# The first projections of a two-layer backbone on one Trainium2 core, with TensorE's order in that stage written out by hand

## The chip, the cores and the metric

The kernel runs on one core of one Trainium2 chip. A core has five engines that work side by side, each through a queue of its own: TensorE (PE, matrix products), VectorE (DVE), ScalarE (ACT), GpSimd (POOL) and SyncE (SP), which in this kernel issues every transfer between memory and the core. An instruction starts when the one ahead of it on its engine has gone and when what it reads and the buffer it writes are free. What counts is the time of one execution on the chip in microseconds (us).

## What is computed

Two layers work on 512 latent and 256 context tokens of 2048 features. Each begins with a normalisation whose scale and shift come from a product of a conditioning vector with a large matrix (the modulation), and then one wide input projection:

```python
for l in range(DEPTH):
    mod = silu_c @ w_mod[l] + b_mod[l]
    shift, scale, gate = jnp.split(mod[:, None, :], 3, axis=-1)
    cmod = silu_cc @ w_mod[l] + b_mod[l]
    cshift, cscale, cgate = jnp.split(cmod, 3)
    h = rmsnorm(x, norm_g[l]) * (1.0 + scale) + shift
    hc = rmsnorm(cx, norm_g[l]) * (1.0 + cscale) + cshift
    if l % 2 == 0:
        u = h @ e_w_in[i]
        uc = hc @ e_w_in[i]
        ...
        y1, yc1 = mixer_a(ua, uca, cs64, lam, lam_init, a_sub_g[i], with_ctx)
        y2, yc2 = mixer_b(ub, ucb, cs128, b_sink[i], with_ctx)
    ...
    y = jnp.concatenate([y1, y2], axis=-1) * jax.nn.silu(ug)
    x = x + gate * (y @ w_o[l])
```

The change lies in the first layer, between the loading of `x` and the first attention head of `mixer_a`: there shift and scale of all 2048 features are needed before `h` is, and four columns of the projection are computed while `h` comes into being. `w_mod[0]` alone is 50 MB.

## The kernel before

The token matrix is held with the features on the 128 partitions: 16 chunks of 128 features, each 128 x 768 (512 latent tokens, then 256 context tokens). All products are float32 worth of precision made of three passes: an operand is split into a rounded part h and a rest l, and `mm_step` (L272) forms h·wh, l·wh and h·wl for the latent columns (512 wide) and the context columns (256 wide), six matmuls in all.

**The first stage** works in eight groups g, each of two chunks, 2g and 2g+1.

- *Modulation of a group*, `mod_first(g)` (L134): shift and scale of 256 features for both conditioning vectors. Its 4.2 MB of weights come in eleven pieces of 384 KB (the last of 256 KB), each loaded on SP's queue (L140) into a buffer called `mraw0`. From each, TensorE makes three narrow matmuls (L144, 32 x 256; 64 rows of the trace to a group) into one accumulator bank T. After the last, ScalarE copies T to an SBUF tile e (L149), four short pairs of matmuls with the constant `sel` pick and add up the result (L151; "the selection", eight rows of the trace), and VectorE adds the bias and forms the scale (`mod_finish`, L125 and L129).
- *h of a chunk*, `make_h` (L342): xn = x times the norm's factor (L348; on VectorE for every third chunk, else on GpSimd), h on ScalarE (L353), then on VectorE the unrounded value (L356) and the rest l (`sub`, L218). It needs the group's shift and scale.
- *Four projected columns* at once (`A_K0`, `A_Q0`, `A_V0`, `E_G0`): four steps of `mm_step` to a chunk, into banks J, J, J, O for the latent tokens and halves of S for the context. Their sums stay open over all 16 chunks. Weights come for four chunks at a time in four pieces of 256 KB (`wraw`, L268; three buffers, and the tile `macc` for the fourth), are rounded by ScalarE (`wh`, L259) and their rest made by VectorE (`wl`, L218), four buffers each.

The pieces `mraw0` live in buffers of two pools: `hslot`, where the h and l of all chunks will be (32 tiles, free until a chunk needs them), for groups 0 to 4, and `slot` (11 tiles), where x lies until its chunk has been normalised, for groups 5 to 7.

**Background work.** The rest of `w_mod` (gates of the first layer, everything of the second) is computed by `mod_later` (L154): 512 KB pieces `mraw` (two buffers of the pool `wp`), multiplied and added up by VectorE (L173) or by ScalarE and GpSimd (L170, L171) in one accumulator `macc`. The generator `later` is advanced by calls of `tick` at many places of the program.

**What sets the order.** The program text is only the dependence order: a scheduler with a timing model places each engine's instructions when the kernel is built, and each engine then runs its list strictly in that order. SP's list holds the transfers, so one whose buffer isn't free yet holds up all behind it. `tc.issue_after(x)` lets the scheduler place an instruction only once x has been placed; `tc.manual_schedule(engines=...)` keeps the named engines' instructions in the order in which the text writes them, within its block. The kernel before has no such block.

## Time and profile before

| | |
|---|---|
| three executions | 2575.84, 2571.32, 2575.29 us; median 2575.29 |
| the profiled execution | 2573.45 us, its span 2571.7 us |
| busy share of the span | TensorE 94%, VectorE 63%, ScalarE 44%, GpSimd 20% |
| moved from and to memory | 297.5 MB, 116 GB/s on average; 326 and 251 GB/s in the first two fortieths of the span |

The page of the profile gives the busy time of each engine over the span, the span in 40 slices of 64 us, and groups of instructions by line. A row of the trace in order of time reads: start, length, engine, line, operation, output<-inputs, tile sizes, how many instructions the row holds, and in brackets how long the engine had been idle before and which instruction ended that. "SPq" rows are transfers that SP issues; a row of waits (engine's queue, line, releaser: total, count, longest) says for what the queue stood still. A row of windows gives, for a stretch of time, each engine's busy time, the clock granted to TensorE (1.00 is full), the share of time that the DMA engines were busy, and GB/s.

### The profile page before, as it was taken

How to read it: one execution, taken by the hardware profiler on the slowest of the kernel's cores; microseconds unless marked ns; L12 is line 12 of the kernel's file. 1: busy time of each engine (PE TensorE's matmuls, PEld its weight loads, DVE VectorE, ACT ScalarE, POOL GpSimd, SP SyncE). 2: the span in 40 equal slices, each digit the busy share in tenths (PEclk: the TensorE clock that was granted, in tenths of full speed). 3: DMA queues.
4: the chain of work that ended last, by engine and by line, in shares of the span. 5: the costliest groups of instructions: out<-in, count | busy, mean ns of one | idle time of the engine just before them, and what ended most of it. 6: DMA issues, size and time to landing. Idle time of an engine off the chain costs nothing.

```text
span 2571.7 us, 36748 instructions
## 1 busy us (share of the span) xinstructions
PE 2427.3 (94%) x14214; PEld 2088.3 (81%) x14214; DVE 1608.2 (63%) x2720; ACT 1128.6 (44%) x2143; POOL 517.6 (20%) x340
## 2 busy tenths in 40 slices
PE   4889999999999999999999999899999999999998
PEld 2667888988788888878878888688888888887787
DVE  4367666656865787877666554857735325776534
ACT  3244444544554554544343332444434334554434
POOL 1132001101400354353303442310010001000010
PEclk9899999999999999999999999899999999999999
DMA  9762111111312233342334554535522222222234
GB/s 326 251 216 74 48 50 56 56 55 57 105 53 69 90 133 124 107 145 97 118 127 153 183 182 138 205 106 170 178 70 79 78 83 70 62 87 70 92 117 148
DMA packets 99087, 297.51 MB, mean 116 GB/s; under 512 B 11616, under 2 KB 12640, under 8 KB 98912
## 3 DMA queue, kind: packets, MB, share of 16 engines
q1 hardware_dynamic: 98912, 295.16, 34.5%
q8 instruction: 112, 1.84, 0.3%
q14 instruction: 63, 0.52, 0.1%
HBM read 269.16 MB, written 25.95 MB: 115 GB/s over the span
## 4 chain that ended last, share of the span: by engine, by line
PE 51%; DVE 7%; issue 2%; ACT 2%; DMA 2%; POOL 1%; ACTq 0%; SPq 0%; DVEq 0%; POOLq 0%
PE J L278 13%; PE J L279 13%; PE J L281 13%; PE O L533 4%; PE S L477 2%; DVE macc L173 2%; PE T L518 2%; DMA mraw<-in_wm_dram 2%; PE S L473 2%; DVE wl L218 1%; POOL macc L171 1%; DVE l L359 1%; DVE mc L489 1%; PE J L181 1%; PE T L243 0%
## 5 line engine op out<-in xcount | busy, mean ns | idle before, releaser
L278 PE MATMUL J<-h,wh 128*128 128x512 f32 (+1 forms) x2224 | 791.3, 359 | 23.8 <-ACT h L353 13.4
L279 PE MATMUL J<-l,wh 128*128 128x512 f32 (+1 forms) x2224 | 769.0, 356 | 4.7 <-DVE l L359 2.7
L281 PE MATMUL J<-h,wl 128*128 128x512 f32 (+1 forms) x2224 | 709.1, 356 | 2.8 <-DVE wl L218 2.8
L218 DVE TENSOR_TENSOR wl<-wraw,wh 128x512 fp32r<-128x512 f32 x500 | 402.2, 809 | 348.2 <-ACT wh L259 326.6
L259 ACT CAST wh<-wraw 128x512 fp32r<-128x512 f32 x492 | 302.4, 618 | 545.2 <-PE J L279 472.1
L278 PEld LDWEIGHTS J<-h,wh 128*128 128x128 f32 x2224 | 424.7, 192 | 104.7 <-ACT h L353 14.5
L279 PEld LDWEIGHTS J<-l,wh 128*128 128x128 f32 x2224 | 426.1, 192 | 62.6 <-DVE l L218 3.9
L281 PEld LDWEIGHTS J<-h,wl 128*128 128x128 f32 x2224 | 390.6, 192 | 38.8 <-DVE wl L218 5.1
L171 POOL TENSOR_TENSOR macc<-macc,mraw 128x512 f32<-128x512 f32 x180 | 267.9, 1489 | 254.1 <-ACT mraw L170 226.6
L278 PE MATMUL J<-yh,wh 128*128 128x512 f32 (+1 forms) x800 | 276.6, 352 | 5.1 <-ACT yh L441 5.1
L279 PE MATMUL J<-yl,wh 128*128 128x512 f32 (+1 forms) x800 | 272.8, 351 | 1.0 <-DVE yl L218 0.9
L173 DVE SCALAR_TENSOR_TENSOR macc<-mraw,silc,macc 128x512 f32<-128x512 f32 x240 | 241.7, 1007 | 42.3 <-DMA mraw<-in_wm_dram 38.6
L281 PE MATMUL J<-yh,wl 128*128 128x512 f32 (+1 forms) x800 | 253.2, 350 | 0.0
L489 DVE TENSOR_REDUCE mc<-S 128x1 f32<-128x768 f32 (+3 forms) x208 | 166.1, 799 | 137.9 <-PE S L477 88.1
L170 ACT ACTIVATE mraw<-mraw,silc 128x512 f32<-128x512 f32 x180 | 129.4, 723 | 192.4 <-DVE macc L173 171.6
L522 ACT CAST pth<-T 128x256 fp32r<-128x256 f32 (+2 forms) x288 | 124.9, 450 | 160.6 <-PE T L518 157.3
L278 PEld LDWEIGHTS J<-yh,wh 128*128 128x128 f32 x800 | 150.9, 190 | 32.8 <-ACT yh L441 5.9
L279 PEld LDWEIGHTS J<-yl,wh 128*128 128x128 f32 x800 | 151.1, 189 | 22.1 <-DVE yl L218 2.8
L218 DVE TENSOR_TENSOR ptl<-T,pth 128x256 fp32r<-128x256 f32 (+2 forms) x288 | 144.5, 514 | 38.6 <-ACT pth L522 35.1
L498 ACT ACTIVATE e<-S,nb 128x256 f32<-128x256 f32 (+3 forms) x144 | 104.3, 724 | 145.1 <-DVE nb L494 102.2
L281 PEld LDWEIGHTS J<-yh,wl 128*128 128x128 f32 x800 | 140.6, 190 | 12.4
L403 POOL TENSOR_TENSOR r<-r,cos 128x512 f32<-128x512 f32 x31 | 44.3, 1429 | 476.3 <-DVE t L402 361.4
(287 smaller groups left out, 3424.7 us busy)
## 6 DMA issues: line engine op xcount, KB each, us to landing
mraw<-in_wm_dram SPq DMA_DIRECT2D x128, 512.0 KB, 3.7
wraw<-in_ew_dram SPq DMA_DIRECT2D x96, 512.0 KB, 3.6
wraw<-in_ow_dram SPq DMA_DIRECT2D x64, 512.0 KB, 3.6
wraw<-in_wo_dram SPq DMA_DIRECT2D x62, 512.0 KB, 3.8
mraw<-in_wm_dram SPq DMA_DIRECT2D x80, 384.0 KB, 7.3
xT<-in_xT_dram SPq DMA_DIRECT2D x16, 384.0 KB, 7.8
res<-in_xT_dram SPq DMA_DIRECT2D x16, 384.0 KB, 4.4
xad<-nx SPq DMA_DIRECT2D x16, 384.0 KB, 2.3
```

Of the source, the lines that this page charges most:

```text
L170: nc.scalar.mul(rv[:, i, :], rv[:, i, :], sc)
L171: nc.gpsimd.tensor_tensor(macc[:, v, :], macc[:, v, :], rv[:, i, :], op=ALU.add)
L173: nc.vector.scalar_tensor_tensor(macc[:, v, :], rv[:, i, :], sc, macc[:, v, :], op0=ALU.mult, op1=ALU.add)
L218: nc.vector.tensor_tensor(o, a, h.bitcast(F32), op=ALU.subtract)
L259: nc.scalar.copy(wh[:, :n, :], rv[:, k0:k0 + n, :])
L278: nc.tensor.matmul(o, lhsT=wh, rhs=xh[:, c0:c1], start=first and (opens or o is lat), stop=False)
L279: nc.tensor.matmul(o, lhsT=wh, rhs=xl[:, c0:c1], start=False, stop=False)
L281: nc.tensor.matmul(o, lhsT=wl, rhs=xh[:, c0:c1], start=False, stop=last and (closes or o is lat))
L489: nc.vector.reduce_max(mc, S, axis=AX.X)
L498: nc.scalar.activation(e, S, AF.Exp, bias=nb, scale=scale, accum_out=den)
L522: nc.scalar.copy(ph, tv)
L533: nc.tensor.matmul(o, lhsT=v[:, cols[i]], rhs=pt[part][:, i, :], start=(n == 0), stop=(n == len(steps) - 1))
```

## The change

Three things are written differently. Nothing is computed differently.

*TensorE's order.* The first stage stands in a block in which TensorE keeps the order of the text, and the text is rearranged. Before, the text drew two pieces of the next group's modulation ahead of each step of the eight of a group, and the scheduler was free. Now, after step 0, 1 and 2 of a group's first chunk come 4, 4 and 3 pieces of the next group's modulation, after step 3 its selection and, in the text, the two h of the next group; then the four steps of the second chunk. For this the generator `mod_first` pauses between ScalarE's copy and the selection, so that one step stands between them.

*Buffers of the pieces.* A table says how many of a group's eleven pieces go into `hslot`: all for groups 0 to 4, 6, 4 and 3 for groups 5, 6 and 7. The others go into `slot`, except the last two of group 7, which take the two `mraw` buffers of the background work.

*The background.* The first two loops of `later` now place their transfers behind `last_raw[0]`, the last piece of the first stage's modulation.

The diff (the file's other lines are the same; the weights of four columns moved into a function of their own, `start_weights`, and the two h into `two_h`):

```diff
         for r0 in range(0, 32, 3):
             n = min(3, 32 - r0)
-            raw = hslot("mraw0", F32) if g < 5 else slot("mraw0")
+            i = r0 // 3
+            if i < (11, 11, 11, 11, 11, 6, 4, 3)[g]:
+                raw = hslot("mraw0", F32)
+            elif g == 7 and i > 8:
+                raw = wp.tile([P, 1024], F32, name="mraw", bufs=2)
+            else:
+                raw = slot("mraw0")
             last_raw[0] = nc.sync.dma_start(raw[:, :n * 256], T["wm0"][g][:, r0 * 256:(r0 + n) * 256])
...
-            yield
+            if r0 + n < 32:
+                yield
         asb = sp["ep"].tile([P, TOK], F32, name="e")[:, 0:512]
         nc.scalar.copy(asb, acc)
+        yield
         for i in range(4):
             nc.tensor.matmul(acc[:, 2 * i:2 * i + 2], lhsT=asb[:, P * i:P * i + P], rhs=sel, start=True, stop=True)
...
         for b in range(8, 12):
-            yield from mod_later(0, b, 2)
+            yield from mod_later(0, b, 2, last_raw[0])
         for b in (4, 5, 6, 7, 0, 1, 2, 3):
-            yield from mod_later(1, b, 2)
+            yield from mod_later(1, b, 2, last_raw[0])
...
-    for _ in mod_first(0):
-        pass
-    for g in range(NCH // 2):
-        nxt = mod_first(g + 1) if g < NCH // 2 - 1 else iter(())
+    def start_weights(k):
+        for i in range(4):
+            raw = sm.tile([P, 2, 512], F32, name="macc", bufs=1).rearrange("p a b -> p (a b)") if i == 3 else None
+            ws4[i] = wsplit(wraw(w, start_cols[i], k, 4, raw), 4)
+
+    def two_h(g):
         for k in (2 * g, 2 * g + 1):
             hs[k] = make_h(0, k, xT[k], rs0, tmp("xn"), "norm")
-        for k in (2 * g, 2 * g + 1):
-            for i, (lat, cx) in enumerate(start_ps):
-                if k % 4 == 0:
-                    raw = sm.tile([P, 2, 512], F32, name="macc", bufs=1).rearrange("p a b -> p (a b)") if i == 3 else None
-                    ws4[i] = wsplit(wraw(w, start_cols[i], k, 4, raw), 4)
-                for _ in range(2):
-                    next(nxt, None)
-                mm_step(lat, cx, ws4[i][k % 4], hs[k], k == 0, k == NCH - 1, opens=(i % 2 == 0), closes=(i % 2 == 1))
-        for _ in nxt:
+
+    with tc.manual_schedule(engines={mybir.EngineType.PE}):
+        for _ in mod_first(0):
             pass
+        two_h(0)
+        for g in range(NCH // 2):
+            nxt = mod_first(g + 1) if g < NCH // 2 - 1 else None
+            for n in range(8):
+                k, i = 2 * g + n // 4, n % 4
+                if k % 4 == 0 and i == 0:
+                    start_weights(k)
+                mm_step(*start_ps[i], ws4[i][k % 4], hs[k], k == 0, k == NCH - 1, opens=(i % 2 == 0), closes=(i % 2 == 1))
+                if nxt is None:
+                    continue
+                if n < 3:
+                    for _ in range((4, 4, 3)[n]):
+                        next(nxt)
+                elif n == 3:
+                    next(nxt)
+                    two_h(g + 1)
```

Lines of the changed kernel are up to 23 higher: the modulation matmul L144 becomes L151, the copy L149 L157, the selection L151 L160, the projection's L278, L279 and L281 become L287, L288 and L290, and VectorE's additions L173 become L182.

**Three places in the lists.** Names carry buffer numbers, which differ between the two programs. In the rows below `T` is the accumulator bank of a group's modulation, `e` its copy, `h0_k` and `l0_k` the two parts of chunk k, `wh` and `wl` those of the weights. A row "x3" is three instructions.

TensorE before, at the end of group 1's modulation, with chunk 2 behind it:

```order
L144 MATMUL T_399<-mraw0_471,sil_185 32x256 x3
L144 MATMUL T_399<-mraw0_482,sil_185 32x256 x3
L144 MATMUL T_399<-mraw0_487,sil_185 32x256 x3
L144 MATMUL T_399<-mraw0_498,sil_185 32x256 x2
L151 MATMUL T_399<-sel_171,e_502 128x2 x4
L278 MATMUL J_308<-h0_2_531,wh_395 128x512
L278 MATMUL J_309<-h0_2_531,wh_418 128x512
L278 MATMUL J_310<-h0_2_531,wh_440 128x512
```

TensorE in the changed kernel, at the end of the same group's modulation:

```order
L151 MATMUL T_425<-mraw0_483,sil_185 32x256 x3
L151 MATMUL T_425<-mraw0_488,sil_185 32x256 x2
L287 MATMUL O_307<-h0_0_379,wh_415 128x512
L288 MATMUL O_307<-l0_0_380,wh_415 128x512
L287 MATMUL S_306<-h0_0_379,wh_415 128x256
L288 MATMUL S_306<-l0_0_380,wh_415 128x256
L290 MATMUL O_307<-h0_0_379,wl_416 128x512
L290 MATMUL S_306<-h0_0_379,wl_416 128x256
L160 MATMUL T_425<-sel_171,e_492 128x2 x4
L287 MATMUL J_308<-h0_1_388,wh_397 128x512
```

Before, the selection followed its last matmul at once and chunk 2, which needs it, came next. Now step 3 of chunk 0 stands between the two, and the steps of chunk 1 behind the selection.

SP's transfers before, from group 7's last pieces on (`cos64` and `sin64` are the tables of the rotary step of the heads, `wraw_1834` and the next two the weights of the first head):

```order
L140 DMA mraw0_1334<-in_wm0_dram 128x768
L140 DMA mraw0_1339<-in_wm0_dram 128x768
L268 DMA wraw_1834<-in_ew_dram 128x1024
L268 DMA wraw_1892<-in_ew_dram 128x1024
L268 DMA wraw_1974<-in_ew_dram 128x1024
L140 DMA mraw0_1350<-in_wm0_dram 128x512
L336 DMA cos64_1447<-in_cos64_dram 128x512
L336 DMA sin64_1449<-in_sin64_dram 128x512
L163 DMA mraw_3552<-in_wm1_dram 128x1024
L163 DMA mraw_3971<-in_wm1_dram 128x1024
```

SP's transfers in the changed kernel, at the same numbers of its list (`mraw0_1278` and the two after it are group 7's first three pieces):

```order
L147 DMA mraw0_1319<-in_wm0_dram 128x768
L147 DMA mraw0_1330<-in_wm0_dram 128x768
L277 DMA wraw_1837<-in_ew_dram 128x1024
L277 DMA wraw_1895<-in_ew_dram 128x1024
L147 DMA mraw0_1278<-in_wm0_dram 128x768
L147 DMA mraw0_1283<-in_wm0_dram 128x768
L147 DMA mraw0_1288<-in_wm0_dram 128x768
L277 DMA wraw_1977<-in_ew_dram 128x1024
L172 DMA mraw_2245<-in_wm1_dram 128x1024
L172 DMA mraw_2836<-in_wm1_dram 128x1024
```

Group 7's first three pieces now stand behind two pieces of the first head's weights, where before only its last one did. The two tables have left this place: they stand early in the new list, beside two pieces of group 7.

VectorE before, around the l of the last two chunks (`modc0` is shift and scale, `macc` the background accumulator):

```order
L173 SCALAR_TENSOR_TENSOR macc_2241<-mraw_3971,silc_181,macc_2241 128x512
L125 TENSOR_TENSOR modc0_193<-T_1251,bmod_174 128x4 x2
L173 SCALAR_TENSOR_TENSOR macc_2241<-mraw_3971,silc_181,macc_2241 128x512
L129 SCALAR_TENSOR_TENSOR modc0_193<-modc0_193,vcol_173 128x4
L356 TENSOR_SCALAR xn_1381<-xn_1381,modc0_193 128x512
L356 TENSOR_SCALAR xn_1381<-xn_1381,modc0_193 128x256
L218 TENSOR_TENSOR l0_14_1384<-xn_1381,h0_14_1383 128x768
L173 SCALAR_TENSOR_TENSOR macc_2241<-mraw_4563,silc_181,macc_2241 128x512
```

VectorE in the changed kernel, at the same l:

```order
L125 TENSOR_TENSOR modc0_193<-T_1277,bmod_174 128x4 x2
L129 SCALAR_TENSOR_TENSOR modc0_193<-modc0_193,vcol_173 128x4
L365 TENSOR_SCALAR xn_1359<-xn_1359,modc0_193 128x512
L365 TENSOR_SCALAR xn_1359<-xn_1359,modc0_193 128x256
L227 TENSOR_TENSOR l0_14_1362<-xn_1359,h0_14_1361 128x768
L182 SCALAR_TENSOR_TENSOR macc_2244<-mraw_2245,silc_181,macc_2244 128x512
L365 TENSOR_SCALAR xn_1368<-xn_1368,modc0_193 128x512
L182 SCALAR_TENSOR_TENSOR macc_2244<-mraw_2836,silc_181,macc_2244 128x512
```

The background additions that stood ahead of the last group's bias now begin behind the l of chunk 14. The first group of background work has fifteen such additions on VectorE in both lists; ahead of the l of chunk 15 stand nine of them before and three now.

## The prediction

> **What bounds the kernel now.** I read the page first, then the first stage in stretches of time, then the rows of three engines in it.
>
> ```profile
> span 2571.7 us, 36748 instructions
> ...
> PE 2427.3 (94%) x14214; PEld 2088.3 (81%) x14214; DVE 1608.2 (63%) x2720; ACT 1128.6 (44%) x2143; POOL 517.6 (20%) x340
> ...
> PEclk9899999999999999999999999899999999999999
> DMA  9762111111312233342334554535522222222234
> ```
>
> TensorE is busy for 94% of the span, and only the first slices (64 us each) show a DMA share of 9, 7 and 6. So most of the program is bound by TensorE and simply moves with the end of the first stage. What the change is worth is read in the first 190 us and in the hand-over behind them.
>
> ```profile
> core 0: us, PE busy (x) PEld busy (x) DVE busy (x) ACT busy (x) POOL busy (x), PEclk, DMA share, GB/s
> 40.00:60.00 20.00, 15.52 (x96) 10.54 (x96) 6.78 (x11) 3.65 (x6) 2.14 (x2) 0.83 0.97 332
> 60.00:80.00 20.00, 17.27 (x100) 11.52 (x101) 8.50 (x13) 4.95 (x8) 2.01 (x1) 0.83 0.78 287
> 100.00:120.00 20.00, 17.87 (x146) 12.42 (x148) 7.59 (x14) 5.57 (x9) 1.84 (x1) 0.91 0.48 170
> ```
>
> No engine is full here. Two things alternate. The first is what the change aims at:
>
> ```profile
> 60.24 0.63 PE L144 MATMUL T<-mraw,sil 128*32 128x256 f32 x6 [0.36 <-DMA mraw<-in_wm_dram]
> ...
> 61.23 1.29 PE L144 MATMUL T<-mraw,sil 128*32 128x256 f32 x10 [0.35 <-DMA mraw<-in_wm_dram]
> ...
> 63.20 1.05 PE L151 MATMUL T<-sel,e 128*128 128x2 f32 x8 [0.69 <-ACT e L149]
> ...
> 65.68 1.65 PE L278 MATMUL J<-h,wh 128*128 128x512 f32 x3 [1.43 <-ACT h L353]
> ...
> 62.00:64.00 2.00, 1.31 (x11) 0.83 (x10) 0.00 (x0) 0.59 (x1) 0.00 (x0) 1.00 1.03 398
> 66.00:68.00 2.00, 2.00 (x6) 1.56 (x6) 1.97 (x5) 1.32 (x3) 0.31 (x1) 0.50 1.03 396
> ...
> 70.00:72.00 2.00, 2.00 (x9) 1.74 (x9) 1.80 (x2) 0.00 (x0) 0.00 (x0) 0.56 0.97 338
> ```
>
> Group 1's last weights are multiplied by 62.5 (61.23 + 1.29). Then TensorE idles 0.69 for the copy, selects for 1.05, idles 1.43 for h, and works at a granted clock of 0.50 until about 71.5. The second is the order of the DMA queue on SP:
>
> ```profile
> SPq L140 <- DVE xn L356: 15.8, 1, 15.8
> SPq L268 <- DVE wl L218: 8.7, 4, 3.3
> ...
> 98.00:100.00 2.00, 2.00 (x17) 0.88 (x17) 0.00 (x0) 0.00 (x0) 0.00 (x0) 1.00 0.06 23
> 108.00:110.00 2.00, 2.00 (x10) 1.67 (x9) 1.97 (x5) 0.00 (x0) 0.00 (x0) 0.68 0.00 0
> 110.00:112.00 2.00, 2.00 (x14) 1.78 (x13) 0.69 (x1) 0.00 (x0) 1.17 (x1) 1.00 0.77 214
> 112.00:114.00 2.00, 2.00 (x13) 1.69 (x12) 0.00 (x0) 0.48 (x1) 0.66 (x1) 1.00 1.07 399
> ```
>
> One transfer at the head of the queue waited 15.8 us for VectorE, and from 98 to 110 nothing was loaded, whatever buffers stood free behind it. The change writes TensorE's order; the waits of SP's queue stay.
>
> **The change part by part.** I follow the ends of the selections. Durations at full clock: a projection step (six matmuls) is 1.05 (the starts of the two rows of 156.50 and 157.55), a chunk of modulation is 0.5 (12 rows, two chunks, in 0.99), so a group of 64 rows 5.3. A chunk (0.39 MB) lands every 0.99 while the queue flows, as the starts 60.24 and 61.23 show.
>
> ```profile
> 142.94 1.06 PE L144 MATMUL T<-mraw,sil 128*32 128x256 f32 x12
> 143.93 0.49 PE L278 MATMUL J<-h,wh 128*128 128x512 f32 x1
> 156.50 0.39 PE L278 MATMUL J<-h,wh 128*128 128x512 f32 x1
> 157.55 0.40 PE L278 MATMUL O<-h,wh 128*128 128x512 f32 x1
> 64.56 0.16 DVE L129 SCALAR_TENSOR_TENSOR modc<-modc,vcol 128x4 f32<-128x4 f32 x1
> 66.60 0.96 DVE L218 TENSOR_TENSOR l<-xn,h 128x768 fp32r<-128x768 f32 x1
> 74.81 0.69 DVE L218 TENSOR_TENSOR wl<-wraw,wh 128x512 fp32r<-128x512 f32 x1 [2.98 <-ACT wh L259]
> 108.43 0.95 DVE L348 TENSOR_TENSOR xn<-xT,e 128x768 f32<-128x768 f32 x1
> 103.76 1.05 PE L151 MATMUL T<-sel,e 128*128 128x2 f32 x8 [0.76 <-ACT e L149]
> ```
>
> Removed: per group the idle 0.69 + 1.43 and about 5.8 us at half clock (65.7 to 71.5, 2.9 us lost), some 5 us. The copy now lies under the fourth step (0.59 under 1.05). Behind the selection stand four steps, 4.2 us, and l is ready 3.3 us after a selection (64.25 to 67.56), so these cover it; without that cover it would cost the 2.1 us of idling again.
>
> Added, on the same path: TensorE now needs a group's chunks one step into the pair of chunks before, not behind them, and so runs into transfers that the old order let finish.
>
> - Group 1: transfers decide as before, its last chunk is used at 62.5. One step, one selection: 64.6 (before 64.25).
> - Group 2: its transfers were queued while the DMA was full (70 to 72: 0.97), so TensorE decides: 8 × 1.05 + 5.3 + 1.05 = 14.8, selection ends 79.4.
> - Group 3: its chunks stand in the queue behind the next weights, two pieces (0.26 MB) and one chunk of group 5, and the first piece waits for a wl that VectorE makes only after h and l: 3.3 + 0.7 = 4.0 behind the selection. The first byte comes 1.5 after a release (VectorE's xn ended 109.38; the 0.43 MB moved by 112 at 0.40 MB per us began at 110.9). Then 0.92 MB take 2.3, and eleven chunks 10.9. With 0.4 for the last rows, a step and a selection: 4.0 + 1.5 + 2.3 + 10.9 + 0.4 + 2.1 = 21.2, selection ends 100.6 (before 104.8). TensorE waits about 3.5 us for the first chunk, then for each.
> - Group 4: a chunk for group 6 waits for xn of chunk 9, which VectorE reaches 4.6 after a selection (104.81 to 109.38). 4.6 + 1.5 + 1.0 + 10.9 + 2.5 = 20.5, so 121.1.
> - Group 5: weights again in front, six own chunks; five lie loaded. 4.0 + 1.5 + 2.3 + 5.9 = 13.7 until the sixth, then 2.5 of rows, two steps and a selection 3.2: 19.4, so 140.5.
> - Group 6: seven chunks lie loaded or in flow, TensorE decides: 14.8, so 155.3.
> - Group 7: its first three chunks stand behind two whole weight pieces (0.52 MB) for the next head, which wait for wl as above. 4.0 + 1.5 + 2.6 + 3.0 = 11.1, then 46 rows 3.8, three steps and a selection 4.2 and 0.5 for a chunk: 19.6, so 174.9.
> - The last three projected chunks: 12 × 1.05 = 12.6, end of the stage 187.5.
>
> ```profile
> 186.73 0.28 PE L281 MATMUL S<-h,wl 128*128 128x256 f32 x1
> 156.19 2.90 SPq L268 DMA_DIRECT2D wraw<-in_ew_dram  x3
> 159.38 0.33 SPq L140 DMA_DIRECT2D mraw<-in_wm_dram  x1
> ```
>
> Before, the stage ends at 187.0, and only group 7's last piece stood behind such weights. So the 20 us or so of removed idling and slow clock come back as waits for chunks: +0.5. The sum's bounds: rows in long runs take 0.06 each instead of 0.08, and a release may pass 0.6 faster or slower; over four loops about ±4.
>
> Two buffers that the background modulation used for its first pieces now hold group 7's last two chunks. Its additions therefore start behind that group instead of at 160.6, and VectorE has three of them before the last l where it had nine.
>
> ```profile
> 160.64 1.53 DVE L173 SCALAR_TENSOR_TENSOR macc<-mraw,silc,macc 128x512 f32<-128x512 f32 x2
> 201.10 1.77 DVE L173 SCALAR_TENSOR_TENSOR macc<-mraw,silc,macc 128x512 f32<-128x512 f32 x1
> 180.00:200.00 20.00, 16.12 (x76) 12.84 (x75) 18.43 (x19) 12.73 (x21) 13.18 (x8) 0.91 0.32 100
> 200.00:220.00 20.00, 14.29 (x80) 12.93 (x79) 19.71 (x20) 8.54 (x15) 8.27 (x6) 0.83 0.26 78
> 220.00:240.00 20.00, 20.00 (x115) 17.42 (x114) 14.41 (x32) 8.87 (x19) 1.63 (x1) 1.00 0.30 105
> 210.52 0.58 PE L278 MATMUL J<-h,wh 128*128 128x256 f32 x1 [5.71 <-ACT r L411]
> ```
>
> From 180 to 220 VectorE is nearly full and TensorE is the one that idles. One addition more falls before head 0's first scores, five more behind them, where VectorE has 5.6 us free in 20. Each takes 0.77 to 1.77. All hidden: 0; none hidden: 6 × 1.77 = 10.6. I take 3, two of them on the path, because the slack covers most of the five.
>
> The new order holds these loads behind a transfer that is itself early in the queue, which costs nothing; the cos and sin tables (0.5 MB) move forward beside group 1 and replace 1.05 MB of background pieces there, so they cost nothing either.
>
> Sum: 0.5 + 3 = +3.5 on the profiled execution's 2573.45 (span 2571.7), so **2577.0**. The shown runs have a median of 2575.29, 1.8 above that execution.
>
> **The rivals.** That the change doesn't do what it says is excluded: the order is fixed when the program is built.
>
> *The queue keeps up.* If releases come earlier than I walk, loops of 19 to 21 us shrink towards TensorE's 14.8. Two of the four: −11, 2566; all: −21, 2556. For it: the DMA moves 399 GB/s when it flows, 4.7 MB per group would need 12 us. Against it: the 15.8 us wait above is of just this kind and stands in the new order too.
>
> *The displaced additions cost their full price.* VectorE's stretch above 9.8 of 10 is longer by 10.6, and head 0's scores and the next head's weights queue behind it: 0.5 + 10.6, 2584.5. It decides from the point where VectorE stays full past head 0's first scores. For it: 19.71 of 20 busy between 200 and 220. Against it: the slack from 220 on.
>
> *The clock falls in the new waits.* Four waits of about 3.5 us each precede a chunk stream; at clock 0.50 six rows take 1.07 (130.25) against the 0.99 between chunks, and a step takes 2.1.
>
> ```profile
> 130.25 1.07 PE L144 MATMUL T<-mraw,sil 128*32 128x256 f32 x6 [0.48 <-DMA mraw<-in_wm_dram]
> ```
>
> If the slow stretch of 5.8 us covers a step that the stream doesn't hide, each wait costs 1 to 2 us more: four times 1.5, 2583. I hold most of it hidden behind the chunks. The Trainium skill ("TensorE: Matmul & The Clock Gate", "Why this matters for your kernels") says to avoid idle gaps of more than about 3 us between bursts, since a window of idling brings the clock back to half. This trace agrees: some 3 us of idling and selecting at 62.5 to 65.7 were followed by 0.50. By that rule the new waits would bring back the slow clock that the change removes.
>
> **How the numbers follow.** A run of this kernel can tell about 0.2% (5.2 us) from no change, so the middle band is 2570.1 to 2580.4. My forecast 0.42, with its own range 2571 to 2583 (0.02 faster, 0.29 same, 0.11 slower); the queue keeps up 0.24 (0.23 faster, 0.01 same); additions at full price 0.20 (0.04 same, 0.16 slower); clock 0.14 (0.08 same, 0.06 slower). Together: faster 0.25, same 0.42, slower 0.33. A tenth left out on each side cuts the second case at about its middle and the high cases at their upper end: 2560 to 2588.
>
> **What would show it.** Right: after h of chunks 4, 6 and 8 no idle for ScalarE and full clock, but idle before the first L151 row of groups 3, 4, 5 and 7 put down to the DMA, with SP waiting for wl or xn; selections ending near 79, 101, 121, 140, 155 and 175; the stage ending within 4 us of 187; the additions beginning near 177. Wrong: DMA share staying near 1 from 75 to 140 and selections every 15 us; or a TensorE idle before head 1's second half much above 5.7 us; or a stage that ends after 192.

## The result, and the profile after

The changed kernel takes 2602.05 us (median of four runs, 2600.94 to 2604.94) against 2574.18 of the kernel before: the ratio is 1.0111, with a 95% interval of 1.0094 to 1.0129. It is 28 us slower. Forecast were 2577.0, within 2560 to 2588.

The span from the page of the changed kernel, and 80 us of its first stage from the view of stretches (start:end, length, busy time of each engine with its instructions, TensorE's granted clock, share of time that the DMA was busy, GB/s):

```profile
span 2599.7 us, 36757 instructions
...
60.00:140.00 80.00, 59.31 (x435) 39.11 (x432) 28.09 (x47) 16.57 (x28) 9.96 (x5) 0.89 0.63 230
```

The same 80 us of the kernel before:

```profile
60.00:140.00 80.00, 70.74 (x488) 47.96 (x489) 28.82 (x49) 17.91 (x29) 9.67 (x5) 0.85 0.75 274
```

TensorE does 11.4 us less work in these 80 us, and the DMA moves less, not more: 230 GB/s for 274. Neither engine works harder; both wait more. For what TensorE waits is told by two rows of the view of waits between 40 and 190 us (who waited, for whom, us in total, times, longest). Before:

```profile
PE T L144 <- DMA mraw<-in_wm_dram: 4.0, 9, 1.0
...
PE J L278 <- ACT h L353: 11.1, 6, 4.3
```

After:

```profile
PE T L151 <- DMA mraw<-in_wm_dram: 33.2, 16, 7.3
...
PE J L287 <- ACT h L362: 3.3, 1, 3.3
```

Of the wait for h only one of 3.3 us is left, ahead of the first group's steps, as the new order meant it to. In its place stand 33 us of waiting for the pieces of the modulation. Here are these waits and the selections that follow them, from TensorE's order of time:

```profile
77.93 0.95 PE L160 MATMUL T<-sel,e 128*128 128x2 f32 x8
...
91.50 3.52 PE L151 MATMUL T<-mraw,sil 128*32 128x256 f32 x24 [7.26 <-DMA mraw<-in_wm_dram]
...
103.91 0.95 PE L160 MATMUL T<-sel,e 128*128 128x2 f32 x8
...
113.89 0.63 PE L151 MATMUL T<-mraw,sil 128*32 128x256 f32 x6 [3.67 <-DMA mraw<-in_wm_dram]
...
126.41 0.95 PE L160 MATMUL T<-sel,e 128*128 128x2 f32 x8
...
139.74 4.14 PE L151 MATMUL T<-mraw,sil 128*32 128x256 f32 x24 [7.01 <-DMA mraw<-in_wm_dram]
...
150.72 0.95 PE L160 MATMUL T<-sel,e 128*128 128x2 f32 x8
...
166.95 0.95 PE L160 MATMUL T<-sel,e 128*128 128x2 f32 x8
...
178.81 3.81 PE L151 MATMUL T<-mraw,sil 128*32 128x256 f32 x24 [5.55 <-DMA mraw<-in_wm_dram]
...
188.92 0.95 PE L160 MATMUL T<-sel,e 128*128 128x2 f32 x8
...
202.97 0.28 PE L290 MATMUL S<-h,wl 128*128 128x256 f32 x1
```

The last row is the end of the stage: 203.25, against 187.0 before. So 16.2 of the 28 us are lost in the stage. The rest comes behind it. A row that both kernels have once for each block of queries and head shows how far the loss has grown: VectorE's product of a denominator with lambda. Here are the first of head 0, the first of head 1 and the last of the eight heads. Before:

```profile
228.39 0.16 DVE L554 TENSOR_TENSOR rd<-rd,nlam 128x1 f32<-128x1 f32 x1
300.55 0.16 DVE L554 TENSOR_TENSOR rd<-rd,nlam 128x1 f32<-128x1 f32 x1
872.85 1.06 DVE L554 TENSOR_TENSOR rd<-rd,nlam 128x1 f32<-128x1 f32 x1
```

After:

```profile
249.09 0.16 DVE L577 TENSOR_TENSOR rd<-rd,nlam 128x1 f32<-128x1 f32 x1
323.93 0.16 DVE L577 TENSOR_TENSOR rd<-rd,nlam 128x1 f32<-128x1 f32 x1
897.68 1.06 DVE L577 TENSOR_TENSOR rd<-rd,nlam 128x1 f32<-128x1 f32 x1
```

20.7, 23.4 and 24.8 us: 4.5 more at the first result of head 0, 2.7 more at that of head 1, 1.4 more by the end of the heads, and 3.2 somewhere behind.

### The profile page after: what moved, and what is told of

Its sections match the earlier page's. It is cut to its first block, busy times and chain, and to the rows that moved or that the text cites. A ratio compares the mean times of both kernels' runs of the same rounds, so it can differ in the third digit from the quotient of the medians.

```text
span 2599.7 us, 36757 instructions
## 1 busy us (share of the span) xinstructions
PE 2428.1 (93%) x14214; PEld 2085.0 (80%) x14214; DVE 1607.5 (62%) x2720; ACT 1128.0 (43%) x2143; POOL 517.9 (20%) x340
## 4 chain that ended last, share of the span: by engine, by line
PE 48%; DVE 8%; DMA 2%; ACT 2%; issue 2%; POOL 1%; ACTq 0%; SPq 0%; DVEq 0%; POOLq 0%
PE J L287 13%; PE J L288 12%; PE J L290 12%; PE O L556 3%; PE S L500 2%; DVE macc L182 2%; DMA mraw<-in_wm_dram 2%; PE T L541 2%; PE S L496 2%; DVE wl L227 1%; DVE l L368 1%; POOL macc L180 1%; DVE mc L512 1%; PE J L190 1%; ACT e L521 0%
## 5 line engine op out<-in xcount | busy, mean ns | idle before, releaser
L287 PE MATMUL J<-h,wh 128*128 128x512 f32 (+1 forms) x2224 | 795.7, 359 | 10.8 <-ACT h L362 5.6
L288 PE MATMUL J<-l,wh 128*128 128x512 f32 (+1 forms) x2224 | 768.8, 355 | 4.4 <-DVE l L368 2.6
L290 PE MATMUL J<-h,wl 128*128 128x512 f32 (+1 forms) x2224 | 708.4, 356 | 8.2 <-DVE wl L227 8.2
L287 PEld LDWEIGHTS J<-h,wh 128*128 128x128 f32 x2224 | 426.1, 192 | 96.8 <-issue 7.4
L288 PEld LDWEIGHTS J<-l,wh 128*128 128x128 f32 x2224 | 426.4, 192 | 58.4 <-DVE l L368 3.4
L290 PEld LDWEIGHTS J<-h,wl 128*128 128x128 f32 x2224 | 391.0, 192 | 43.3 <-DVE wl L227 10.8
L287 PE MATMUL J<-yh,wh 128*128 128x512 f32 (+1 forms) x800 | 275.5, 351 | 4.5 <-ACT yh L464 4.5
L182 DVE SCALAR_TENSOR_TENSOR macc<-mraw,silc,macc 128x512 f32<-128x512 f32 x240 | 246.4, 1027 | 53.6 <-DMA mraw<-in_wm_dram 49.8
L288 PE MATMUL J<-yl,wh 128*128 128x512 f32 (+1 forms) x800 | 271.9, 350 | 1.2 <-DVE yl L227 0.9
L290 PE MATMUL J<-yh,wl 128*128 128x512 f32 (+1 forms) x800 | 253.0, 349 | 0.0
L287 PEld LDWEIGHTS J<-yh,wh 128*128 128x128 f32 x800 | 150.1, 189 | 31.7 <-ACT yh L464 5.3
L521 ACT ACTIVATE e<-S,nb 128x256 f32<-128x256 f32 (+3 forms) x144 | 104.2, 724 | 153.9 <-DVE nb L517 111.2
L288 PEld LDWEIGHTS J<-yl,wh 128*128 128x128 f32 x800 | 150.6, 189 | 22.4 <-DVE yl L227 3.3
L290 PEld LDWEIGHTS J<-yh,wl 128*128 128x128 f32 x800 | 140.2, 189 | 12.7 <-DVE wl L227 0.2
```

The costliest lines, as they stand in the source:

```text
L182: nc.vector.scalar_tensor_tensor(macc[:, v, :], rv[:, i, :], sc, macc[:, v, :], op0=ALU.mult, op1=ALU.add)
L287: nc.tensor.matmul(o, lhsT=wh, rhs=xh[:, c0:c1], start=first and (opens or o is lat), stop=False)
L288: nc.tensor.matmul(o, lhsT=wh, rhs=xl[:, c0:c1], start=False, stop=False)
L290: nc.tensor.matmul(o, lhsT=wl, rhs=xh[:, c0:c1], start=False, stop=last and (closes or o is lat))
L521: nc.scalar.activation(e, S, AF.Exp, bias=nb, scale=scale, accum_out=den)
```

## The experiments

The selections' ends, in us, are the measure of the stage in all of them (start of the row plus its length, as above; where a trace splits a selection into two rows, the end of the later one). Each ratio is to executions of the kernel before in the same session:

| kernel | g2 | g3 | g4 | g5 | g6 | g7 | end of the stage | median, ratio to before (95%) |
|---|---|---|---|---|---|---|---|---|
| before | 84.9 | 104.8 | 127.2 | 139.8 | 160.3 | 171.9 | 187.0 | |
| forecast | 79.4 | 100.6 | 121.1 | 140.5 | 155.3 | 174.9 | 187.5 | 2577.0 |
| changed | 78.9 | 104.9 | 127.4 | 151.7 | 167.9 | 189.9 | 203.2 | 2602.05, 1.0111 (1.0094 to 1.0129) |
| order alone | 79.8 | 105.5 | 128.0 | 143.2 | 157.0 | 170.8 | 185.5 | 2578.61, 1.0016 (1.0005 to 1.0027) |
| buffers alone | 85.3 | 105.0 | 127.5 | 147.3 | 164.2 | 182.7 | 195.2 | 2590.98, 1.0060 (1.0044 to 1.0077) |
| weights behind | 77.6 | 102.1 | 125.7 | 148.8 | 170.1 | 193.3 | 206.7 | 2603.55, 1.0107 (1.0087 to 1.0127) |
| group 7 in slots | 78.1 | 103.8 | 126.8 | 152.2 | 168.4 | 191.6 | 206.1 | 2597.88, 1.0086 (1.0070 to 1.0103) |
| queue in order | 71.2 | 85.0 | 98.8 | 112.6 | 126.3 | 140.1 | 152.8 | 2554.46, 0.9929 (0.9914 to 0.9944) |
| order and queue, old buffers | 71.0 | 84.8 | 98.6 | 112.3 | 126.1 | 142.0 | 154.7 | 2555.16, 0.9928 (0.9912 to 0.9943) |
| before and queue | 80.4 | 105.2 | 124.6 | 144.9 | 162.3 | 178.0 | 191.0 | 2591.53, 1.0070 (1.0053 to 1.0087) |
| clock kept | 78.4 | 104.0 | 127.1 | 150.5 | 166.6 | 187.6 | 201.0 | 2599.73, 1.0112 (1.0092 to 1.0131) |
| pieces in order | 77.2 | 101.8 | 115.6 | 140.1 | 153.9 | 177.0 | 190.4 | 2591.15, 1.0069 (1.0052 to 1.0086) |
| queue in order, background held | 70.4 | 84.1 | 97.9 | 111.7 | 125.4 | 139.2 | 151.9 | 2561.46, 0.9948 (0.9933 to 0.9963) |
| changed, background held | 78.1 | 103.7 | 126.4 | 149.5 | 165.6 | 188.4 | 201.1 | 2607.29, 1.0125 (1.0110 to 1.0140) |
| background in the stage | 69.7 | 84.3 | 99.0 | 113.6 | 129.1 | 145.1 | 158.7 | 2561.98, 0.9956 (0.9943 to 0.9969) |

### Which part of the change costs it

Two theories. *Queue*: the pieces are late because a transfer that stands ahead of them on SP waits for something. *Buffers*: the table and the two borrowed tiles are the cause. The written order by itself could also cost it all. The change's halves were run alone. The first has TensorE's new order with the old buffers, and the background's placing as before:

```diff
-            i = r0 // 3
-            if i < (11, 11, 11, 11, 11, 6, 4, 3)[g]:
-                raw = hslot("mraw0", F32)
-            elif g == 7 and i > 8:
-                raw = wp.tile([P, 1024], F32, name="mraw", bufs=2)
-            else:
-                raw = slot("mraw0")
+            raw = hslot("mraw0", F32) if g < 5 else slot("mraw0")
...
-            yield from mod_later(0, b, 2, last_raw[0])
+            yield from mod_later(0, b, 2)
```

> TensorE's order alone: the pieces lie in the buffers of the kernel before, and the background is placed as before. Queue theory (the late groups are those whose pieces stand behind weights that wait for wl): group 3 still stands behind two pieces of weights, so its selection stays near 105 and the stage ends 8 to 16 us later than the 187.0 before; the additions are early again, so nothing is lost behind the stage: 2582 to 2592. Buffer theory (the table and the two borrowed buffers are the cause): stage within 3 us of 187, 2571 to 2578. If the written order costs all of it by itself: 2598 to 2605.

The order alone takes 2578.61 us, 0.16% more than before, and its stage ends at 185.5. The time is within a microsecond of what the buffer theory expected; but groups 3 and 4 wait as in the changed kernel, as the queue theory has it. Groups 5 to 7 don't: their rows follow without an idle ahead.

```profile
104.51 0.95 PE L154 MATMUL T<-sel,e 128*128 128x2 f32 x8
...
114.42 0.63 PE L145 MATMUL T<-mraw,sil 128*32 128x256 f32 x6 [3.60 <-DMA mraw<-in_wm_dram]
...
133.32 1.50 PE L145 MATMUL T<-mraw,sil 128*32 128x256 f32 x24
...
148.49 1.50 PE L145 MATMUL T<-mraw,sil 128*32 128x256 f32 x24
...
162.27 1.50 PE L145 MATMUL T<-mraw,sil 128*32 128x256 f32 x24
```

Group 5's pieces now go into slots and are loaded as x's chunks leave these, before they are used; a wait of the queue later on does them no harm. The second run has the new buffers with the old text and the old freedom of the scheduler (the first stage's loop of the kernel before, under the new table).

> The new buffers of the pieces alone, with TensorE's order left to the scheduler and the text as before. Queue theory: TensorE needs each group's pieces late, so the stage ends within 4 us of 187.0; the additions start later, as group 7's last pieces lie in their buffers, and cost 3 to 7 us behind it: 2576 to 2584. Buffer theory: 2595 to 2603. If the additions behind the stage cost nothing: 2571 to 2577.

It is 0.60% slower (2590.98) and its stage ends at 195.2, between the two theories' expectations. It hardly waits for pieces (3.2 us); the waits for the copy and for h are 14.2 us against 8.9 before in the stage from 60 us on (4.3 and 9.9; 2.1 and 6.8). So under this queue the buffers harm both orders. The third part of the change, the background's `issue_after`, does nothing: without it every engine's list is the same as with it.

### Is it the weights' wait for wl?

That was the forecast's step for groups 3, 5 and 7. The stage's weights were put behind the last piece of the group whose loop comes before:

```diff
-            ws4[i] = wsplit(wraw(w, start_cols[i], k, 4, raw), 4)
+            with tc.issue_after(last_raw[0].ins) if k else nullcontext():
+                piece = wraw(w, start_cols[i], k, 4, raw)
+            ws4[i] = wsplit(piece, 4)
```

> The changed kernel with the stage's weights (chunks 4, 8 and 12) placed behind the last piece of the group whose loop comes before, so that no piece waits behind a weight that waits for wl; the first head's weights stay where they are. Queue theory: group 3's selection near 94 instead of 104.9, group 5 no longer 24 us behind group 4 but 15 to 18, the stage ends 14 to 20 us earlier than 203.2, 2582 to 2590. Clock theory (the half clock after a wait is what costs) or too little bandwidth: other waits take their place, under 5 us gained, 2597 to 2603.

Nothing was gained (2603.55). The stage's weights no longer wait for wl (from 70 to 160 us SP has no such wait; the 8.2 us that it has later are for the first head's weights), but SP waits for other releases, in the view of its waits from 70 to 210 us:

```profile
SPq L147 <- POOL xn L357: 21.1, 2, 11.3
SPq L147 <- PE T L151: 20.2, 4, 10.0
SPq L147 <- DVE xn L365: 14.6, 1, 14.6
```

In the changed kernel the same view had 40.2 us for wl (seven waits, the longest 12.2), 19.5 for TensorE, 12.5 for VectorE's xn and 3.2 for GpSimd's. A piece of group 6, whose slot comes free only when xn of a later chunk is made, stands ahead of group 3's pieces and took the wait over. The theory that the weights alone are the cause falls. The other cut, every piece behind the one used before it and the weights left where they are, leaves only the waits for wl:

```diff
-            last_raw[0] = nc.sync.dma_start(raw[:, :n * 256], T["wm0"][g][:, r0 * 256:(r0 + n) * 256])
+            with tc.issue_after(last_raw[0].ins) if last_raw[0] is not None else nullcontext():
+                last_raw[0] = nc.sync.dma_start(raw[:, :n * 256], T["wm0"][g][:, r0 * 256:(r0 + n) * 256])
```

> The changed kernel with every piece behind the one used before it, so that nothing that waits for xn stands ahead of an earlier piece; the weights stay where they are, so two of them, waiting for wl, stand ahead of groups 3, 5 and 7. If those weights alone cost what the changed kernel pays: selections of groups 3, 5 and 7 come 22 to 25 us behind the one before, those of groups 4 and 6 14 us, the stage ends at 186 to 194, 2583 to 2593. If the pieces that wait for xn were the whole cost: 14 to 16 us apart everywhere, the stage ends before 165, 2553 to 2560.

The stage ends at 190.4. Groups 3, 5 and 7 come 24.6, 24.5 and 23.1 us behind the one before, groups 4 and 6 13.8, as the first of the two expectations had it. Here are groups 3 to 5:

```profile
76.28 0.95 PE L161 MATMUL T<-sel,e 128*128 128x2 f32 x8
88.26 1.07 PE L152 MATMUL T<-mraw,sil 128*32 128x256 f32 x6 [5.67 <-DMA mraw<-in_wm_dram]
...
100.86 0.95 PE L161 MATMUL T<-sel,e 128*128 128x2 f32 x8
...
114.64 0.95 PE L161 MATMUL T<-sel,e 128*128 128x2 f32 x8
...
126.44 2.10 PE L152 MATMUL T<-mraw,sil 128*32 128x256 f32 x12 [5.49 <-DMA mraw<-in_wm_dram]
...
139.14 0.95 PE L161 MATMUL T<-sel,e 128*128 128x2 f32 x8
```

So a weight that waits for wl does cost a group some 10 us; and with it gone, in the run before, the next wait ahead cost as much. What counts is that something waits ahead, not what.

### The whole queue in the order of use

Both cuts together, and the tables and first head's weights behind group 7's last piece:

```diff
+    gate = [None]
+
     def wraw(w, col, k0, nk, raw=None):
...
-        nc.sync.dma_start(raw[:, :nk * P], w[col // P][:, k0 * P:(k0 + nk) * P])
+        with tc.issue_after(gate[0].ins) if gate[0] is not None else nullcontext():
+            nc.sync.dma_start(raw[:, :nk * P], w[col // P][:, k0 * P:(k0 + nk) * P])
...
     with tc.issue_after(last_raw[0].ins):
         load_cs(64)
+    gate[0] = last_raw[0]
```

> The changed kernel with its buffers, but the queue in the order of use: every piece behind the one used before it, the stage's weights behind the last piece of the group before, the tables and the first head's weights behind group 7's last piece. The run with the weights alone behind gained nothing, since the next transfer ahead, a piece for group 6 that waits for xn, took the wait over. Queue theory (any transfer that waits ahead of a piece, whatever it waits for): selections 15 to 17 us apart, the stage ends near 170 to 178, 2568 to 2580 with the additions still late. Buffer theory (group 5, 6 and 7 wait for h-buffers that come free only as TensorE uses the pieces in them): group 5 and later stay 19 to 24 us apart, the stage ends after 190, 2588 to 2600.

2554.46 us, a ratio of 0.9929 (0.9914 to 0.9944): faster than before, and 48 us faster than the changed kernel with the same order on TensorE and the same buffers. The stretch from 60 to 140:

```profile
60.00:140.00 80.00, 80.00 (x708) 57.72 (x706) 39.29 (x65) 22.82 (x40) 13.88 (x7) 1.00 0.94 334
```

TensorE never idles there and its clock is full; selections come some 13.8 us apart; the stage ends at 152.8. The expectation's 170 to 178 was too careful: from 60 us to the end of the stage TensorE waits for nothing. The same queue with the old buffers:

> TensorE's new order with the old buffers and the queue in the order of use. Queue theory: selections 15 to 16 us apart, the stage ends at 166 to 172 instead of 185.5 with the new order alone, and 12 to 18 us of it reach the end: 2558 to 2568. Buffer theory: the first groups gain, groups 5 to 7 wait for x's buffers; the stage ends at 175 to 185, 2568 to 2578.

2555.16 us and 154.7, below both expectations: the buffers, which cost 17.7 us of stage under the scheduler's queue (203.2 against 185.5), cost nothing under this one. They are no cause by themselves; they decide which pieces are exposed to the queue's waits. And the queue without TensorE's order, in the kernel before:

> The kernel before, TensorE's order left to the scheduler, with the queue in the order of use. If the queue is what bounds both kernels: the idle for pieces goes and what is left is the idle for the copy and h and the slow clock; selections 18 to 20 us apart, the stage ends at 176 to 184, 2563 to 2572. If TensorE's order is needed to use it: within 3 us of 187 and of 2573.

2591.53 us, slower than before by 0.70% (0.53 to 0.87), and beyond both expectations; the stage ends 4 us later than before, and the rest is lost behind it. TensorE's waits for h (6.4 us) and the copy (3.2) remain between 60 and 240, pieces wait 53.1 us for TensorE to free their buffers, and 8.1 us go to a wait for vl behind the stage. Neither half helps alone; the two together give about 18 us.

### The slow clock

In the changed kernel the first 24 rows after a wait take 4.14 us (139.74) where 24 rows take 1.50 at full clock. To ask what that costs, extra products fill the waits and keep the clock up:

```diff
+        for _ in range((0, 0, 0, 24, 10, 24, 0, 20)[g]):
+            nc.tensor.matmul(acc, lhsT=hs[0][0][:, 0:P], rhs=hs[0][0][:, 0:512], start=True, stop=True)
         for r0 in range(0, 32, 3):
...
```

> The changed kernel, with 24, 10, 24 and 20 extra products of 512 columns ahead of the first piece of groups 3, 4, 5 and 7, into the bank that the group's own products then overwrite; they fill most of the waits, so the clock stays up. Nothing else is changed. Theory of the slow clock as a price: in groups 4, 5 and 7 the rows and the step behind the wait took about 2.1, 3.6 and 2.8 us more than at full clock and no piece was waited for behind them; if the pieces are there, the stage ends 6 to 9 us earlier, 2593 to 2597. If the pieces only land as fast as the slow rows use them: under 2 us, 2600 to 2604, with short idles for pieces in place of slow rows.

The stage ends 2.3 us earlier in its trace, nearer the second expectation than the first. In the times nothing of it can be told: the ratio is 1.0112 (1.0092 to 1.0131), that of the changed kernel 1.0111. Group 5's rows then run fast and wait for each piece:

```profile
132.28 5.63 PE L139 MATMUL T<-h 128*128 128x512 f32 x24
...
139.37 0.63 PE L154 MATMUL T<-mraw,sil 128*32 128x256 f32 x6 [1.46 <-DMA mraw<-in_wm_dram]
140.34 0.63 PE L154 MATMUL T<-mraw,sil 128*32 128x256 f32 x6 [0.34 <-DMA mraw<-in_wm_dram]
```

So the slow rows were mostly hidden behind the landing of the pieces. The Trainium skill ("TensorE: Matmul & The Clock Gate", "Why this matters for your kernels") would have idle gaps of over about 3 us avoided for the clock's sake; the clock did fall to 0.50 in these waits, but keeping it up gained only 2.3 us of the stage.

### The additions behind the stage

Between the end of the stage and head 0's first result, VectorE's background additions alone, in the view of stretches (stretch, length, busy time with count, clock, DMA). Before:

```profile
187.00:228.40 41.40, 5.04 (x4) 0.88 0.31 100
```

After:

```profile
203.20:249.10 45.90, 9.69 (x9) 0.81 0.30 95
```

Five more additions, 4.65 us more, and the stretch is 4.5 longer. VectorE as a whole is busy for 38.8 of these 41.4 us before and for 44.4 of 45.9 after: it has hardly room for them there. As a test, group 7's last two pieces went back into slots and the background's transfers were no longer placed behind them, so that it has its buffers from the start:

```diff
-            elif g == 7 and i > 8:
-                raw = wp.tile([P, 1024], F32, name="mraw", bufs=2)
...
-            yield from mod_later(0, b, 2, last_raw[0])
+            yield from mod_later(0, b, 2)
...
-            yield from mod_later(1, b, 2, last_raw[0])
+            yield from mod_later(1, b, 2)
```

> The changed kernel, but group 7's last two pieces lie in slots again and the background has its own two buffers from the start. Theory of the displaced additions: the stage ends near 203 as it does now, and the 7 us that head 0 loses against the stage's end come back: 2593 to 2597. Rival (the head is late for another reason, as its tables or weights): 2600 to 2604.

2597.88 us: 4.2 less than the changed kernel, though its stage ends 2.9 later. Head 0's first result comes 14.4 us later than before, with a stage 19.1 later; the last of the heads 17.6. So their early place was worth 7 us by the medians (4.2 and 2.9; the intervals of the two ratios still overlap a little), and up to 10 by the heads in the traces (the changed kernel loses 8.6 behind the stage, this one gains 1.5). From the end of the stage to head 0's first result it has two additions (3.67 us) in 36.7 us, 9.2 less than the changed kernel, of which the additions make 6.0; what makes the other 3 was not traced.

Holding them back instead doesn't help. The background's first loop was put behind the last weights that the program has asked for when that loop begins, those of head 1, first in the run with the queue in order, then in the changed kernel (`mod_later(0, b, 2, last_w[0])`, with `last_w[0]` set at each load of weights):

> The run with the changed kernel's buffers and the queue in the order of use, whose stage ends 34 us earlier than before though only 18 us reach the end; here the background's first loop is also held behind the weights of head 1, so that no addition stands in VectorE's list beside head 0. Theory of the displaced additions: VectorE is full from 160 to 180 in that run and TensorE idles 7.6 us of those 20; without the additions most of that idle goes, 2545 to 2550. Rival (VectorE's work is only moved and stops TensorE later instead): 2552 to 2558.

> The changed kernel with the background's first loop held behind the weights of head 1; the stage isn't touched, so it ends at 202 to 206. Theory of the displaced additions: the 7 us that head 0 loses behind the stage go, and some more, as head 0 has fewer additions than in the kernel before: 2590 to 2596. Rival (moved, not removed): 2599 to 2604.

2561.46 (0.9948, 0.9933 to 0.9963) and 2607.29 (1.0125, 1.0110 to 1.0140): neither is faster than without, and both lie above the ranges of both theories. In the first, head 0's first result comes 42.8 us earlier than in the kernel before, head 1's only 19.8:

```profile
185.59 1.26 DVE L585 TENSOR_TENSOR rd<-rd,nlam 128x1 f32<-128x1 f32 x1
...
280.78 0.16 DVE L585 TENSOR_TENSOR rd<-rd,nlam 128x1 f32<-128x1 f32 x1
```

The lead of 42.8 has shrunk to 27.5 by the third result of head 0; around it, from 198 to 232 us, TensorE waits 4.0 us for VectorE's e (L587). The work was moved and stopped TensorE later. The other way round, six pieces of the background were put into the stage of the run with order, queue and old buffers, one behind each of groups 2 to 7:

```diff
...
                 elif n == 3:
                     next(nxt)
                     two_h(g + 1)
+                    if g in (1, 2, 3, 4, 5, 6):
+                        behind_now[0] = last_raw[0]
+                        next(bg)
+                        due[0] += 1
+                        due[1] += 1
...
```

> The run with TensorE's new order, the old buffers and the queue in the order of use, with six pieces of the background put into the stage, one behind the last piece of each of groups 2 to 7 (the fourth weight piece lies in a tile that the heads use later, as the background needs its accumulator). VectorE is busy for 5 to 14 of each 20 us there. If what the heads lose is VectorE's work that the short stage no longer holds (18 of 34 us reach the end; holding the additions back moved the loss without ending it): eleven additions of 0.75 to 1.9 us leave the full stretch, the stage stays at 152 to 157, 2540 to 2549 against 2555. Rival (the place of the additions doesn't matter, or the 3 MB more in the queue delay the pieces as much as they save): 2551 to 2558.

2561.98 (0.9956, 0.9943 to 0.9969), a miss by both. The stage grew by 4 us (158.7; TensorE waits 3.9 us for l, as VectorE has more to do), and head 0 was quick: head 1's first result came 30.7 us earlier than in the kernel before, against 14.9 in the run without. But three results later this had shrunk to 14.4:

```profile
269.84 0.16 DVE L586 TENSOR_TENSOR rd<-rd,nlam 128x1 f32<-128x1 f32 x1
324.90 0.89 DVE L586 TENSOR_TENSOR rd<-rd,nlam 128x1 f32<-128x1 f32 x1
```

(the second row's like stands at 339.30 in the kernel before). What takes it away there was not traced. The scheduler places all that follows anew in each of these kernels, and their lead over the kernel before wanders by 10 us and more on the way through the layer. So of the 34 us that the ordered stage gains about 18 reach the end, and what it would take to keep more stays open.

## Why the prediction was wrong

The trace ends 28.0 us later than before where 3.5 were forecast. Of the 24.5 us missed, 15.7 lie in the stage (16.2 for 0.5), 5.6 between its end and the heads' last result (8.6 for 3), and 3.2 behind the heads.

**The mechanism of the waits was right, its size was not.** The forecast walked from selection to selection; here are its intervals and what they became.

| interval | forecast | measured |
|---|---|---|
| g1 to g2 | 14.8 | 13.8 |
| g2 to g3 | 21.2 | 26.0 |
| g3 to g4 | 20.5 | 22.5 |
| g4 to g5 | 19.4 | 24.3 |
| g5 to g6 | 14.8 | 16.2 |
| g6 to g7 | 19.6 | 22.0 |
| g7 to the end | 12.6 | 13.4 |

Every wait is where the forecast put it, on the transfer that it named (only the piece ahead of group 3's is one of group 6 in SP's list, not of group 5, of the same size), and each is longer. The step of the sum that failed is "the first byte comes 1.5 after a release ... then 0.92 MB take 2.3". From the end of the selection to the first row of the group it gives 8.8, 8.1, 8.8 and 9.1 us for groups 3, 4, 5 and 7. Measured are 12.6, 9.0, 12.4 and 10.9 (91.50 less 78.88, and so on): 10.1 of the 15.7 us by which the stage was missed. Two things lengthen it. Here is group 3's case, VectorE, GpSimd, SP and then stretches of one us:

```profile
82.10 2.94 DVE L227 TENSOR_TENSOR wl<-wraw,wh 128x512 fp32r<-128x512 f32 x2
82.31 2.17 POOL L357 TENSOR_TENSOR xn<-xT,e 128x768 f32<-128x768 f32 x1 [11.74 <-DVE l L227]
82.81 0.33 SPq L277 DMA_DIRECT2D wraw<-in_ew_dram  x1
85.06 0.33 SPq L277 DMA_DIRECT2D wraw<-in_ew_dram  x1
85.48 8.26 SPq L147 DMA_DIRECT2D mraw<-in_wm_dram  x12
...
85.00:86.00 1.00, 0.00 (x0) 0.00 (x0) 1.00 (x4) 0.00 (x0) 0.00 (x0) 1.00 0.04 16
86.00:87.00 1.00, 0.00 (x0) 0.00 (x0) 1.00 (x3) 0.00 (x0) 0.00 (x0) 1.00 0.63 195
87.00:88.00 1.00, 0.00 (x0) 0.00 (x0) 0.88 (x2) 0.00 (x0) 0.00 (x0) 0.81 0.60 103
88.00:89.00 1.00, 0.00 (x0) 0.00 (x0) 0.00 (x0) 0.00 (x0) 0.98 (x1) 0.50 0.86 259
```

The first release came 3.9 after the selection (82.81), as forecast (4.0). But the forecast let both weight pieces go at once; the second waited 2.25 more for its own wl. And the flow began slowly: 195, 103 and 259 GB/s in the three us from 86 on, where the forecast had 1.5 us and then the full rate of 400. The twelve pieces of the row at 85.48 begin with group 6's; group 3's own first was issued at 85.96, and its first row came 5.5 later (91.50). Group 5 has both delays too (its weights went at 131.29 and 133.54). Group 7 has only the slow start: its two weights went 0.6 apart, its own first piece at 172.77, and its first row came 6.0 after that, 1.8 more in all than forecast, as against 3.8 and 3.6 in groups 3 and 5. The page of the kernel before has a line for the time from issue to landing of such pieces (count, size, median):

```profile
mraw<-in_wm_dram SPq DMA_DIRECT2D x80, 384.0 KB, 7.3
```

The forecast read the spacing of landings in a full stream instead. (The median holds pieces issued into a full queue as well, so it isn't the price of a start by itself.) The rest is spread: 1.0 less in group 2, whose 64 narrow rows were reckoned at 5.3 us and take about 4 (24 take 1.50), 1.1 to 1.4 more in groups 4, 5 and 6, and so on.

**"So the 20 us or so ... come back as waits for chunks: +0.5" held for half of the change, and that by chance.** With the old buffers the same order ends the stage at 185.5 and the run at 2578.61, near what was forecast for the whole, with longer waits in groups 3 and 4 and none in 5 and 7. The walk had the table's cost in it (group 5's "six own chunks", group 7's first three behind the next head's weights) but never asked what these groups would cost without it: 15.2 instead of 24.3 us for group 5, 13.9 instead of 22.0 for group 7.

**The additions.** The second term, 3 of up to 10.6 us, was too small. Five more additions stand before head 0's first result, 4.65 us, and that result comes 4.5 later against the stage's end; by the end of the heads 8.6 us are lost behind the stage. The rival of the additions at full price had the right mechanism and nearly the right sum, and "the slack covers most of the five" was the wrong choice: before, VectorE had 2.6 us free ahead of head 0's first result (38.8 busy of 41.4), not the 5.6 that the forecast read between 220 and 240, most of which lie behind it. How much of the 4.1 us lost between that result and the last of the heads is the additions' was not traced.

**The other rivals.** *The queue keeps up* gave 2556 for all four loops: what stood against it was true of this change. The run that puts the queue in order reached 2554.46, but that the numbers agree is chance: its stage is 34 us shorter, not 21, and only 18 reach the end. *The clock*: keeping it up gained 2.3 us of stage, as against the 6 of its rival; holding most of it hidden was right. That the order does what it says was right: no idle for h is left behind group 0's.

**The range** ended at 2588. Its upper cases were each reckoned alone on a stage that ends at 187; a stage 16 us later and additions at nearly full price together were not in it. "A stage that ends after 192" was named as what would prove it wrong.

The remaining 3.2 us behind the heads were not traced. In the trace of the order alone the last result of the heads is 5.2 us later than before, and its end 7.3, so something of the kind is not special to the changed kernel.

## What to carry to other kernels

An order written out for the engine that computes is only as good as the order of the queue that feeds it: written alone it cost 0.2%, the queue alone cost 0.7%, both together gained 0.7%. When one waiting transfer is moved out of the way, look at what stands ahead next, since taking away only the named wait left the time as it was here. And where a transfer starts from rest, take the time from issue to landing, not the spacing of a full stream; and price work that is pushed into an engine's full stretch at its whole length.

## What the runs showed of the hardware

*VectorE behind GpSimd.* The two wl of 82.10 took 2.94 us with GpSimd's xn beside them, and in the same trace, with no GpSimd row beside them, two took 1.28:

```profile
171.08 1.28 DVE L227 TENSOR_TENSOR wl<-wraw,wh 128x512 fp32r<-128x512 f32 x2
```

The second of the first pair ended 0.56 after GpSimd's row did (85.04, and 82.31 + 2.17 = 84.48), about the length of one wl: it looks as if it stood still until then. The Trainium skill ("SBUF — State Buffer", "SBUF: two separate sides") says that a VectorE operation with two inputs in SBUF and a GpSimd operation exclude each other for the whole instruction. These rows agree.

*A stream from rest.* Once the queue flows, a piece lands about every 0.97 to 0.99 us (the rows at 139.37 and 140.34 above, and those of the prediction). Behind a standstill of the queue, the first row came 5.5 us (group 3) and 6.0 us (group 7) after the group's own first piece was issued, with the weights and, in group 3, another piece ahead.

*The clock* fell to 0.50 some 3 to 4 us after TensorE's last step in group 3's wait: its steps end at 84.24, the stretch from 87 to 88 has 0.81, the next 0.50.
